# A scan layer without a state between its two chunks, and the decay's differences of three of its groups on ScalarE

## The chip, the cores and the metric

The kernel runs on one core of a Trainium2 chip. A core has engines that each work through a queue of their own in order: TensorE (matmul, "PE" in the profile, its weight loads "PEld"), VectorE ("DVE"), ScalarE ("ACT"), GpSimd ("POOL") and SyncE ("SP", here only the issuer of weight transfers). They wait for one another through semaphores; an instruction that waits holds up everything behind it on its engine. Operands lie in SBUF; TensorE writes into eight PSUM banks of 128 x 512 float32, from which VectorE and ScalarE read.

The metric is device time in microseconds (us) of one execution, as the median of the runs.

## The reference

A decoder trunk of two layers for 256 tokens of width 1024: SwiGLU, a mixer, SwiGLU again, with a layer norm after each. The mixer of the first layer is sparse attention, that of the second a state-space scan (Mamba-2) in two chunks of 128 tokens, 32 heads of 64 in four groups that share B and C (128 states). Only the scan is touched:

```python
xdt = x * dt                                   # (chunk, token, group, head, 64)
a_cs = cumsum(dt * a)                          # within the chunk
decay = exp(where(tril, a_cs[l] - a_cs[s], -inf))
cb = einsum('bclgn,bcsgn->bcgls', cm, bm)
y_diag = einsum('bcgrls,bcsgrp->bclgrp', cb * decay, xdt)
states = einsum('bclgn,bclgrp->bcgrpn', bm, xdt * decay_to_end)
prev = scan of the states over the chunks      # zero for the first chunk
y_off = einsum('bclgn,bcgrpn->bclgrp', cm, prev) * exp(a_cs)
y = y_diag + y_off
```

With two chunks only the second has a nonzero `prev`, and it is the state of the first. So `y_off` of the second chunk is C2 (B1' X1), where B1' X1 is the state and X1 is `xdt * decay_to_end` of the first chunk. The same numbers come from (C2 B1') X1.

## The kernel before

Weights are streamed as 512 KB tiles: SyncE loads them, ScalarE rounds each into a high half (`wh`, L327, or L325 with a scale) and VectorE forms the rest (`wl`, L352, or L349); TensorE multiplies with both. Up to ten tiles are ready ahead of their use. The order on every engine is written by hand: instructions are queued as the Python code calls them.

The scan layer is the function `ssd`. It first projects z, B and C (`z0`, `z_half`, `bc_tile`), then transposes B (`b_tr`, L1467) and multiplies C with B for both chunks (`cb`, L1473). Then it loops over four groups of eight heads (L1636). A tile of x comes from `xs_tile` (a projection, then a conv of one ScalarE instruction, L1449, and three VectorE ones, L1452, and a silu, L1444). For a group g and a chunk t:

- `x_tok` transposes x into tokens and multiplies with dt (L1523, `y[t]`, tile `xdt`) and with the skip factor (L1524, tile `xtok`); `x_end` (L1528) gives X1, tile `xe`.
- `decay_load` broadcasts the cumulated sums into `M` by a transfer of GpSimd; `decay_seg` (L1499) subtracts each of eight heads' column sum, 128 x 128 at a time, and clips at zero, on VectorE; `decay_exp` (L1502) is one exp of 128 x 1024 on ScalarE; `decay_cb` (L1506) multiplies with C times B on VectorE. The `seg`, `exp` and `cb` of group g + 1 are queued in the last part of group g.
- `diag` (L1534) is the diagonal product; `state` (L1540) forms the state from the transposed B (`btok`) and X1 and copies it to SBUF on ScalarE (L1542); `carry` (L1546) multiplies it with C2, and VectorE adds it (L1547, L1548).
- `gate` (L1551, L1552) adds the skip part and multiplies with silu(z); `square`, `root`, `norm` (L1556, L1559, L1563) are the group's RMS norm; `y_tr` (L1568) transposes y on TensorE, and `split_psum` (L526, L527) makes its two halves, `yH` on ScalarE and `yL` on VectorE.

Between these steps stand eight fillers f[0] to f[7], pieces of TensorE work for the next group: x tiles, halves of z, or pieces of the output product. `diag`, `carry`, the second `x_tok` and `y_tr` share two PSUM banks (`ptr`).

Of the kernel before, what the change touches and what calls it, by code (L numbers as in the profile page):

```python
# [408 lines left out]
def trunk_kernel(ctx: ExitStack, tc: tile.TileContext, widths, forms, x, ln_g, ln_b, wts, kvg, convp,  # L409
                 dt_bias, a_log, d_skip, norm_g, out):  # L410
    nc = tc.nc
# [10 lines left out]
    def nm(s):  # L422
        cnt[0] += 1
        return f"{s}_{cnt[0]}"

    def f4(s):
        return wk.tile([128, 1024], F32, name=nm(s), tag="f4", bufs=12)

    def f2(s):
        return wk.tile([128, 512], F32, name=nm(s), tag="f2", bufs=9)  # L430
# [18 lines left out]
    def pspare(n):  # L449

        spare[0] = (spare[0] + 1) % (n + 2)
        if spare[0] < 2:
            return pmm()
        a, b = divmod(spare[0] - 2, 2)
        return psum.tile([128, 512], F32, name=nm("psp"), tag=f"acc{a}{b}", bufs=1)

    def ptr():
        return psum.tile([128, 512], F32, name=nm("ptr"), tag="ptr", bufs=2)
# [20 lines left out]
    ident = consts.tile([128, 128], F32, name="ident")  # L479
# [850 lines left out]
    def ssd(xT, u, ln_i):  # L1330
# [108 lines left out]
        bT, cTt = f4("bT"), f4("cTt")  # L1439
# [22 lines left out]
            W.pump(1 + i % 2)  # L1462

        cbm = f4("cbm")
        btok = f2("btok")

        def b_tr():  # L1467
            pt = pspare(4)
            for g in range(SG):
                nc.tensor.transpose(pt[:, g * 128:(g + 1) * 128], bT[:, g * 256:g * 256 + 128], ident)  # L1470
            nc.scalar.copy(btok, pt)

        def cb(t):  # L1473
            pt = pspare(4)
# [15 lines left out]
        def decay_seg(t, g, on_act=False):  # L1490

            m = M[t, g]
            for h in range(8):
                hs = slice(h * 128, (h + 1) * 128)
                a = acs[t][:, g * 8 + h:g * 8 + h + 1]
                if on_act:
                    nc.scalar.activation(m[:, hs], m[:, hs], AF.Relu, bias=a, scale=-1.0)
                else:
                    nc.vector.tensor_scalar(m[:, hs], m[:, hs], a, 0.0, op0=ALU.subtract, op1=ALU.min)  # L1499

        def decay_exp(t, g, on_act=False):
            nc.scalar.activation(M[t, g], M[t, g], AF.Exp, scale=-1.0 if on_act else 1.0)  # L1502
# [4 lines left out]
                                 .to_broadcast([128, 8, 128]))  # L1507

        yT = {}
        y, xd, xe, st, ss = {}, {}, {}, {}, {}  # L1510

        def x_tok(t, g):

# [21 lines left out]
                                 y[t][:, h * 64:(h + 1) * 64], start=True, stop=True)  # L1535
            return py

        def state(g):
            pst = ptr()
            nc.tensor.matmul(pst, btok[:, g * 128:(g + 1) * 128], xe[g], start=True, stop=True)  # L1540
            st[g] = f2("st")
            nc.scalar.copy(st[g], pst)  # L1542

        def carry(g):
            po = ptr()
            nc.tensor.matmul(po, cTt[:, g * 256 + 128:g * 256 + 256], st[g], start=True, stop=True)  # L1546
            nc.vector.tensor_mul(hv(xe[g]), hv(po), hb(eacs, g))  # L1547
            nc.vector.tensor_add(xd[1], xd[1], xe[g])  # L1548

# [69 lines left out]
        for i in range(4):  # L1619
            xs_tile(0, i, u + i)  # L1620
            if i == 0:
                b_tr()
                cb(0)
                cb(1)
        decay_seg(0, 0)
# [10 lines left out]
        for g in range(SG):  # L1636
            if g < 2:
                f = [lambda i=i: xs_tile(g + 1, i, u + i) for i in range(4)]
                f += [lambda t=t, i=i: (z_half(g + 2, t, i, u + 4), W.pump(1)) for t in range(2) for i in range(2)]
            elif g == 2:  # L1640
                x3 = [lambda i=i: xs_tile(3, i, u + 2 * i) for i in range(4)]
                o0 = [lambda i=i: out_piece(i, u + 2 * i + 1) for i in range(4)]
                f = [x3[0], x3[1], o0[0], x3[2], o0[1], x3[3], o0[2], o0[3]]
            else:
                f = [lambda i=i: out_piece(4 + i, u + i) for i in range(6)]
            f[0]()
            if g:
                x_tok(0, g)
                x_tok(1, g)
            else:  # L1650
                decay_cb(0, 0)
                decay_cb(1, 0)
            x_end(g)
            f[1]()
            f[2]()
            py[0] = diag(0, g)
            state(g)
            gate(0, g, py[0])
            if g < 3:
                decay_load(0, g + 1)  # L1660
            f[3]()
            carry(g)
            square(0)
            root(0)
            py[1] = diag(1, g)
            gate(1, g, py[1])
            if g < 3:
                decay_load(1, g + 1)
            f[4]()
            square(1)  # L1670
            root(1)
            norm(0)
            if g < 3:
                decay_seg(0, g + 1)
            f[5]()
            y_tr(0, g)
            norm(1)
            if g < 3:
                decay_seg(1, g + 1)
                f[6]()  # L1680
                flush()
                y_tr(1, g)
                decay_exp(0, g + 1)
                decay_exp(1, g + 1)
                f[7]()
                decay_cb(0, g + 1)
                decay_cb(1, g + 1)
                W.lows()
                u += 8
# [56 lines left out]
```

## Time and profile before

| what | us |
|---|---|
| median of 3 runs (lowest, highest) | 1030.28 (1030.23, 1030.36) |
| span of the profiled execution (first to last instruction) | 1029.3 |
| TensorE busy in the span | 1014.3 |
| VectorE busy | 882.6 |
| ScalarE busy | 637.4 |
| from the first group's x tiles to the last group's second y_tr, about | 696 to 829 |

The profiled execution's own time isn't listed apart from its span; the median of the runs is 1.0 us above the span, and that is taken as what lies around it. "Busy" is an engine's time in instructions; matmuls overlap, so that a row's duration is longer than the distance to the next row's start, and the same holds for VectorE and ScalarE, by some 0.1 us. In the order of time a row gives start, duration, engine, source line, operation, written tile <- read tiles, shape and count; brackets give how long the engine was idle just before and what ended that.

### The profile page before, as it was taken

To read this page: it belongs to the slowest core of one execution; us is meant where nothing else is said; L and a number is where in the kernel's file an instruction comes from. 1 tells how busy PE (TensorE), PEld (TensorE's weight loads), DVE (VectorE), ACT (ScalarE), POOL (GpSimd) and SP (SyncE) were. 2 spreads that over 40 slices of the span, in tenths; PEclk is the share of its full clock that TensorE was granted. 3 is DMA by queue.
4 is the path that set the end of the run, shared out by engine and by line. 5 is a ranking of instruction groups with operands and counts; after the bars stand their busy time and mean duration, and the time that the engine had idled before them with its cause. 6 is when DMAs were issued, how large, how long until landed. Compare 5 with 4: busy or idle time off the path is not lost.

```text
span 1029.3 us, 14864 instructions
## 1 busy us (share of the span) xinstructions
PE 1014.3 (99%) x5427; PEld 861.6 (84%) x5427; DVE 882.6 (86%) x1305; ACT 637.4 (62%) x977; POOL 94.8 (9%) x152
## 2 busy tenths in 40 slices
PE   8999999999999999999999999999999999999996
PEld 7888888888788888888888888999888888888885
DVE  5889997799799799978978997799999878898984
ACT  6666675476657666754666664586766547566760
POOL 2011000100000010000001000140111110101001
PEclk9999999999999999999999999999999999999998
DMA  9769998352658677884777787355555656678741
GB/s 328 289 142 287 268 330 291 105 172 75 203 186 243 182 201 234 307 305 133 236 205 191 246 295 255 138 170 185 181 167 193 213 207 222 150 234 278 208 156 41
DMA packets 60776, 217.55 MB, mean 211 GB/s; under 512 B 6848, under 2 KB 6912, under 8 KB 60704
## 3 DMA queue, kind: packets, MB, share of 16 engines
q1 hardware_dynamic: 51264, 183.43, 50.5%
q0 software_dynamic: 9152, 32.66, 15.3%
q8 instruction: 42, 0.69, 0.3%
q10 hardware_dynamic: 288, 0.52, 0.1%
q14 instruction: 30, 0.25, 0.1%
HBM read 193.48 MB, written 1.08 MB: 189 GB/s over the span
## 4 chain that ended last, share of the span: by engine, by line
PE 93%; DVE 4%; DMA 1%; ACT 0%; POOL 0%; issue 0%; SPq 0%; POOLq 0%; DVEq 0%
PE pmm L532 11%; PE pmm L530 11%; PE pmm L531 11%; PE acc L530 10%; PE acc L532 10%; PE acc L531 9%; PE pmm L679 4%; PE ptr L679 4%; PE ptr L681 2%; PE pmm L681 2%; PE ptr L531 1%; PE ptr L532 1%; PE pxs L530 1%; PE ptr L530 1%; PE pxs L532 1%; PE pxs L531 1%
## 5 line engine op out<-in xcount | busy, mean ns | idle before, releaser
L352 DVE TENSOR_TENSOR wl<-raw,wh 128x1024 fp32r<-128x1024 f32 (+2 forms) x404 | 475.4, 1212 | 16.0 <-ACT wh L327 15.6
L327 ACT CAST wh<-raw 128x1024 fp32r<-128x1024 f32 (+2 forms) x406 | 407.4, 1045 | 100.8 <-DVE raw L294 46.6
L530 PE MATMUL acc<-wh,hH 128*128 128x512 f32 (+1 forms) x352 | 137.7, 391 | 0.0
L532 PE MATMUL acc<-wh,hL 128*128 128x512 f32 (+1 forms) x352 | 136.6, 388 | 0.0
L531 PE MATMUL acc<-wl,hH 128*128 128x512 f32 (+1 forms) x352 | 136.6, 388 | 0.0
L530 PE MATMUL pmm<-wh,xT 128*128 128x512 f32 (+2 forms) x288 | 114.6, 398 | 0.0
L531 PE MATMUL pmm<-wl,xT 128*128 128x512 f32 (+2 forms) x288 | 110.8, 385 | 0.8 <-DVE wl L352 0.8
L532 PE MATMUL pmm<-wh,xT 128*128 128x512 f32 (+2 forms) x288 | 111.2, 386 | 0.2 <-DVE xT L527 0.2
L532 PEld LDWEIGHTS acc<-wh,hL 128*128 128x128 f32 x352 | 66.1, 188 | 13.7
L530 PEld LDWEIGHTS acc<-wh,hH 128*128 128x128 f32 x352 | 66.2, 188 | 12.7
L531 PEld LDWEIGHTS acc<-wl,hH 128*128 128x128 f32 x352 | 66.2, 188 | 12.6
L532 PE MATMUL pmm<-wh,xf 128*128 128x512 f32 x192 | 74.8, 389 | 0.0
L530 PE MATMUL pmm<-wh,xf 128*128 128x512 f32 x192 | 74.7, 389 | 0.0
L531 PE MATMUL pmm<-wl,xf 128*128 128x512 f32 x192 | 74.7, 389 | 0.0
L267 POOL DMA_DIRECT2D raw<-raw x42 | 36.5, 869 | 410.3 <-DVE raw L294 149.6
L294 DVE TENSOR_TENSOR raw<-raw,raw 128x1024 f32<-128x1024 f32 x54 | 65.2, 1219 | 0.4
L532 PEld LDWEIGHTS pmm<-wh,xT 128*128 128x128 f32 x288 | 54.2, 188 | 12.4 <-DVE xT L527 1.5
L531 PEld LDWEIGHTS pmm<-wl,xT 128*128 128x128 f32 x288 | 54.4, 189 | 10.7 <-DVE wl L352 1.4
L530 PEld LDWEIGHTS pmm<-wh,xT 128*128 128x128 f32 x288 | 54.3, 189 | 9.3 <-ACT wh L327 0.4
L679 PE MATMUL pmm<-xT,wh 128*128 128x512 f32 x192 | 49.3, 399 | 0.0
L679 PE MATMUL ptr<-xT,wh 128*128 128x512 f32 x192 | 47.9, 392 | 0.0
L530 PE MATMUL pxs<-xT,wh 128*128 128x256 f32 x160 | 46.4, 290 | 0.0
(313 smaller groups left out, 1897.6 us busy)
## 6 DMA issues: line engine op xcount, KB each, us to landing
raw<-in_wts_dram SPq DMA_DIRECT2D x339, 512.0 KB, 5.1
raw<-raw POOLq DMA_DIRECT2D x42, 512.0 KB, 5.2
M<-scr POOLq DMA_DIRECT2D x8, 512.0 KB, 5.1
lng<-in_ln_g_dram POOLq DMA_DIRECT2D x6, 512.0 KB, 5.1
lnb<-in_ln_b_dram POOLq DMA_DIRECT2D x6, 512.0 KB, 6.3
raw<-in_wts_dram SPq DMA_DIRECT2D x4, 408.0 KB, 5.3
out_dram<-x SPq DMA_DIRECT2D x4, 256.0 KB, 2.1
raw<-in_wts_dram SPq DMA_DIRECT2D x2, 492.0 KB, 4.8
```

The costliest lines, as they stand in the source:

```text
L267: self.nc.gpsimd.dma_start(self.raw[r], self.raw[other], accum_op=ALU.add)
L294: self.nc.vector.tensor_add(self.raw[r], self.raw[r], self.raw[other])
L327: nc.scalar.copy(h[:, c:c + n], raw[:, c:c + n])
L352: self.nc.vector.tensor_sub(lo[:, s], raw[:, s], h[:, s].bitcast(F32))
L530: nc.tensor.matmul(ps, lh, rh, start=first, stop=False, skip_group_check=on)
L531: nc.tensor.matmul(ps, lh, rl, start=False, stop=False, skip_group_check=on)
L532: nc.tensor.matmul(ps, ll, rh, start=False, stop=last, skip_group_check=on)
L679: nc.tensor.matmul(ps, H[:, k * 128:(k + 1) * 128], xT.HL[:, k, :], start=k == 0, stop=False)
L681: nc.tensor.matmul(ps[:, :SEQ], L[:, k * 128:(k + 1) * 128], xT.H[:, k, :], start=False, stop=k == DK - 1)
```

## The change

The state goes. Instead of transposing B of the first chunk, TensorE multiplies it with C of the second, once for all four groups (`cb_cross`), and ScalarE copies the result to SBUF (`cbx`). `carry` then multiplies `cbx` with X1, so that `state` (a matmul of 128 x 512 and a ScalarE copy per group) is left out. And for groups 2 to 4 (g + 1 in the loop) the eight differences of a chunk are computed on ScalarE, as Relu(a - M) with the sums as a bias; the exp then takes a scale of -1. Both functions had that path (`on_act`) already. Group 1 stays on VectorE.

```diff
         cbm = f4("cbm")
-        btok = f2("btok")
-
-        def b_tr():
+        cbx = f2("cbx")
+
+        def cb_cross():
             pt = pspare(4)
             for g in range(SG):
-                nc.tensor.transpose(pt[:, g * 128:(g + 1) * 128], bT[:, g * 256:g * 256 + 128], ident)
-            nc.scalar.copy(btok, pt)
+                nc.tensor.matmul(pt[:, g * 128:(g + 1) * 128], bT[:, g * 256:g * 256 + 128],
+                                 cTt[:, g * 256 + 128:g * 256 + 256], start=True, stop=True)
+            nc.scalar.copy(cbx, pt)
...
-        def state(g):
-            pst = ptr()
-            nc.tensor.matmul(pst, btok[:, g * 128:(g + 1) * 128], xe[g], start=True, stop=True)
-            st[g] = f2("st")
-            nc.scalar.copy(st[g], pst)
-
         def carry(g):
             po = ptr()
-            nc.tensor.matmul(po, cTt[:, g * 256 + 128:g * 256 + 256], st[g], start=True, stop=True)
+            nc.tensor.matmul(po, cbx[:, g * 128:(g + 1) * 128], xe[g], start=True, stop=True)
...
             if i == 0:
-                b_tr()
+                cb_cross()
                 cb(0)
                 cb(1)
...
             py[0] = diag(0, g)
-            state(g)
             gate(0, g, py[0])
...
             norm(0)
             if g < 3:
-                decay_seg(0, g + 1)
+                decay_seg(0, g + 1, True)
             f[5]()
             y_tr(0, g)
             norm(1)
             if g < 3:
-                decay_seg(1, g + 1)
+                decay_seg(1, g + 1, True)
                 f[6]()
                 flush()
                 y_tr(1, g)
-                decay_exp(0, g + 1)
-                decay_exp(1, g + 1)
+                decay_exp(0, g + 1, True)
+                decay_exp(1, g + 1, True)
```

Three places in the queues show what moves. The first is ScalarE at the end of group 1, from the first norm on (`xdt` is y, `zs` silu of z, `wh` a weight tile's high half, `M` the decay). Before:

```order
L1563 ACTIVATE xdt_7128<-xdt_7128,rs_7332 128x512
L1430 ACTIVATE zs_7394<-pmm_7347 128x512
L327 CAST wh_7399<-raw_7263 128x1024
L526 CAST yH_7407<-ptr_7402 128x512
L1563 ACTIVATE xdt_7137<-xdt_7137,rs_7371 128x512
L327 CAST wh_7436<-raw_7318 128x1024
L1444 ACTIVATE xsT_7310<-cv_7311 128x256
L526 CAST yH_7445<-ptr_7440 128x512
L1502 ACT_TABLE_LOAD
L1502 ACTIVATE M_7283<-M_7283 128x1024
```

In the changed kernel the same stretch reads:

```order
L1558 ACTIVATE xdt_7128<-xdt_7128,rs_7328 128x512
L1498 ACTIVATE M_7279<-M_7279,acs_6849 128x128 x8
L1430 ACTIVATE zs_7390<-pmm_7343 128x512
L327 CAST wh_7395<-raw_7263 128x1024
L526 CAST yH_7403<-ptr_7398 128x512
L1558 ACTIVATE xdt_7137<-xdt_7137,rs_7367 128x512
L1498 ACTIVATE M_7341<-M_7341,acs_6851 128x128 x8
L327 CAST wh_7432<-raw_7314 128x1024
L1444 ACTIVATE xsT_7306<-cv_7307 128x256
L526 CAST yH_7441<-ptr_7436 128x512
L1503 ACT_TABLE_LOAD
L1503 ACTIVATE M_7279<-M_7279 128x1024
```

Eight instructions of 128 x 128 stand behind each of the two norms; nothing else has changed its place, and the number of table loads is the same. The second place is VectorE at the same point of the program, from the root of the second chunk to the products with C times B. Before:

```order
L1559 TENSOR_SCALAR ss_7366<-ss_7366 128x1
L1499 TENSOR_SCALAR M_7283<-M_7283,acs_6849 128x128 x8
L352 TENSOR_TENSOR wl_7364<-raw_7225,wh_7363 128x1024
L527 TENSOR_TENSOR yL_7408<-ptr_7402,yH_7407 128x512
L1499 TENSOR_SCALAR M_7345<-M_7345,acs_6851 128x128 x8
L352 TENSOR_TENSOR wl_7400<-raw_7263,wh_7399 128x1024
L527 TENSOR_TENSOR yL_7446<-ptr_7440,yH_7445 128x512
L352 TENSOR_TENSOR wl_7437<-raw_7318,wh_7436 128x1024
L1506 TENSOR_TENSOR M_7283<-M_7283,cbm_6374 128x1024
L1506 TENSOR_TENSOR M_7345<-M_7345,cbm_6374 128x1024
L352 TENSOR_TENSOR wl_7468<-raw_7361,wh_7467 128x1024
```

And in the changed kernel:

```order
L1554 TENSOR_SCALAR ss_7362<-ss_7362 128x1
L352 TENSOR_TENSOR wl_7360<-raw_7225,wh_7359 128x1024
L527 TENSOR_TENSOR yL_7404<-ptr_7398,yH_7403 128x512
L352 TENSOR_TENSOR wl_7396<-raw_7263,wh_7395 128x1024
L527 TENSOR_TENSOR yL_7442<-ptr_7436,yH_7441 128x512
L352 TENSOR_TENSOR wl_7433<-raw_7314,wh_7432 128x1024
L1507 TENSOR_TENSOR M_7279<-M_7279,cbm_6374 128x1024
L1507 TENSOR_TENSOR M_7341<-M_7341,cbm_6374 128x1024
L352 TENSOR_TENSOR wl_7464<-raw_7357,wh_7463 128x1024
```

The two runs of eight are gone; what is left reads, row by row, something that ScalarE has just written (`wh`, `yH`, `M`). The third place is TensorE behind the first diagonal product of group 1 (`pxs` is the next x tile). Before:

```order
L532 MATMUL pxs_7230<-xT_6313,wl_6892 128x256
L1534 MATMUL ptr_7268<-xdt_7128,M_6853 128x64 x8
L1540 MATMUL ptr_7277<-xe_7190,btok_6375 128x512
L530 MATMUL pxs_7285<-xT_6313,wh_6928 128x256
L531 MATMUL pxs_7285<-xT_6313,wh_6928 128x256
```

And in the changed kernel:

```order
L532 MATMUL pxs_7230<-xT_6313,wl_6892 128x256
L1535 MATMUL ptr_7268<-xdt_7128,M_6853 128x64 x8
L530 MATMUL pxs_7281<-xT_6313,wh_6928 128x256
L531 MATMUL pxs_7281<-xT_6313,wh_6928 128x256
L532 MATMUL pxs_7281<-xT_6313,wl_6929 128x256
```

The state product has left the queue, and the x tile follows the diagonal directly; `carry` keeps its place behind the x tile.

More of the change, by code (lines that the diff above doesn't have):

```diff
@@ L1509, in ssd @@
         yT = {}
-        y, xd, xe, st, ss = {}, {}, {}, {}, {}
+        y, xd, xe, ss = {}, {}, {}, {}
         def x_tok(t, g):
```

## The prediction

> **What bounds the kernel now.** I read the page first, then the waits of TensorE, then the order of time engine by engine between 690 and 830 us, the stage that the change touches. The first row is the page's busy time (us, share of the span, instructions); the next two are rows of the waits (who waited for whom, us in total, times, longest); the fourth is ten microseconds of that stage (PE, PEld, DVE, ACT, POOL busy, then clock).
>
> ```profile
> PE 1014.3 (99%) x5427; PEld 861.6 (84%) x5427; DVE 882.6 (86%) x1305; ACT 637.4 (62%) x977; POOL 94.8 (9%) x152
> ...
> PE ptr L1534 <- DVE xdt L1551: 0.8, 1, 0.8
> ...
> PE pxt L1521 <- ACT xsT L1444: 0.7, 1, 0.7
> ...
> 740.00:750.00 10.00, 10.00 (x79) 9.68 (x78) 9.24 (x13) 8.75 (x11) 0.00 (x0) 1.00 0.60 196
> ```
>
> TensorE is the bound: 1.5 us of waits in the whole scan layer, both in its first group. So an instruction taken from TensorE is worth its time, but only as long as VectorE (9.24 of 10 us) and ScalarE (8.75 of 10) keep up. ScalarE's 62% is an average; in this window it is nearly full, and the change adds to it there.
>
> **Term 1, TensorE's instructions.** Rows of the chain of work (start, us, what):
>
> ```profile
> 696.26 0.44 PE psp L1470 x4
> 696.70 1.91 PE pmm L1477 x16
> ...
> 782.68 0.91 PE ptr L1540 x2
> ```
>
> The state product of a group (L1540) goes: 0.91 us each, four times, 3.64 us. The four transposes (0.44 us) become four products of the form of L1477, which are two instructions each: 1.91 / 8 = 0.24 us each, 0.96 in all, so +0.52. The fourth now needs the last C tile, which a ScalarE row dates (start, us):
>
> ```profile
> 696.76 0.41 ACT L1444 ACTIVATE cTt<-cv 128x256 f32<-128x256 f32 x1
> ```
>
> The tile is ready at 697.17, the fourth product would start at 696.98: about 0.2 more. TensorE, then VectorE behind it, are on the chain until group 1's second diagonal, so this +0.7 is paid in full.
>
> **Term 2, the moved differences.** Eight 128x128 VectorE instructions (row 735.00 below) take 1.65 us; ScalarE has no Relu of 128x128 in this trace. The nearest form is L1166: same size, in place, a per-partition bias, scale -1 (its accumulator read is a row of its own):
>
> ```profile
> 231.00 0.39 ACT L1166 ACTIVATE lg<-lg,mx 128x128 f32<-128x128 f32 x1
> 231.29 0.19 ACT L1166 ACTIVATION_READ_ACCUMULATOR lg<-lg,mx 128x1 f32 x1
> ```
>
> The next instruction starts 0.29 us after it. Bounds: 0.18 (in the rows below a silu of 512 columns without a bias pointer starts its successor after 0.50 us and a cast of 1024 after 0.93; that slope leaves 0.18 for 128) and 0.39 (no overlap at all). I take 0.29, the row of the same form: eight are 2.3 us, sixteen 4.6 us per group, for groups 2 to 4. The removed state copy (0.58 us of ScalarE) lies where ScalarE waits anyway: nothing.
>
> Where they stand decides. Group 1's end on ScalarE:
>
> ```profile
> 734.54 0.71 ACT L1563 ACTIVATE xdt<-xdt,rs 128x512 f32<-128x512 f32 x1
> 735.36 0.60 ACT L1430 ACTIVATE zs<-pmm 128x512 f32<-128x512 f32 x1
> 735.86 1.04 ACT L327 CAST wh<-raw 128x1024 fp32r<-128x1024 f32 x1
> 736.79 0.59 ACT L526 CAST yH<-ptr 128x512 fp32r<-128x512 f32 x1
> 737.27 0.74 ACT L1563 ACTIVATE xdt<-xdt,rs 128x512 f32<-128x512 f32 x1
> ...
> 744.92 1.04 ACT L327 CAST wh<-raw 128x1024 fp32r<-128x1024 f32 x1
> ```
>
> From the first norm to the cast at 744.92 ScalarE has only some 0.3 us of gaps, so sixteen more instructions push that cast by 4.4 us. VectorE and TensorE behind it (start, us, what, and in brackets the idle time before):
>
> ```profile
> 735.00 1.65 DVE L1499 TENSOR_SCALAR M<-M,acs 128x128 f32<-128x128 f32 x8
> ...
> 745.99 1.23 DVE L352 TENSOR_TENSOR wl<-raw,wh 128x1024 fp32r<-128x1024 f32 x1 [0.69 <-ACT wh L327]
> ...
> 748.56 0.68 DVE L1523 TENSOR_TENSOR xdt<-pxt,dt 128x512 f32<-128x512 f32 x1
> ...
> 756.72 0.69 DVE L1551 TENSOR_TENSOR xdt<-ptr,xtok 128x512 f32<-128x512 f32 x1
> ...
> 778.47 0.68 DVE L1523 TENSOR_TENSOR xdt<-pxt,dt 128x512 f32<-128x512 f32 x1
> ...
> 785.28 0.69 DVE L1551 TENSOR_TENSOR xdt<-ptr,xtok 128x512 f32<-128x512 f32 x1
> ```
>
> ```profile
> 727.80 2.00 PE L1534 MATMUL ptr<-xdt,M 128*128 128x64 f32 x16 [0.75 <-DVE xdt L1551]
> 738.57 0.60 PE L1568 MATMUL ptr<-ident,xdt 128*128 128x128 f32 x4
> ...
> 757.62 1.89 PE L1534 MATMUL ptr<-xdt,M 128*128 128x64 f32 x16
> ...
> 768.22 0.60 PE L1568 MATMUL ptr<-ident,xdt 128*128 128x128 f32 x4
> ```
>
> Times below are those of before; "+" is how much later an event comes, the 0.7 of term 1 apart.
>
> Group 1. First norm ends 735.17 as now. Eight Relus to 737.5, then silu 0.49, cast 0.93, yH 0.47: the second norm starts at 739.4 and ends at 740.1. The transposes of y(1) stand at 738.57 and need it: **+1.6** on TensorE. Eight more Relus and the rest unchanged: the cast of 744.92 comes at 749.3. VectorE is 3.2 us lighter but does not get ahead: it waits in program order for yH(1), for both exponentials, then for that cast, as it does already (0.69 us in brackets at 745.99). So L1523 comes at 752.9, +4.4, and the 8.2 us from there to L1551 hold no idle time: gate(0) also +4.4. The second diagonal of group 2 waits for it (its bank is the one that gate(0) reads): now it starts 0.2 us after L1551 ends at 757.41, so **+4.2**. The state product taken out of TensorE before it buys only a wait, here as in group 1, where the row at 727.80 waits for L1551 already.
>
> Group 2 has the same tail:
>
> ```profile
> 764.21 0.71 ACT L1563 ACTIVATE xdt<-xdt,rs 128x512 f32<-128x512 f32 x1
> ...
> 774.17 0.60 ACT L1430 ACTIVATE zs<-pmm 128x512 f32<-128x512 f32 x1
> ```
>
> Its norm hangs on VectorE, +4.4. Relus (769.2 to 771.5), silu, a cast of 1.04, yH: the second norm ends at 774.3, so y(1)'s transposes of 768.22 come **+6.1**. After the next eight Relus, the table load and the exponentials the silu of 774.17 ends at 783.5. TensorE's next x tile uses the PSUM bank that it reads:
>
> ```profile
> 775.09 0.36 PE L530 MATMUL pmm<-xT,wh 128*128 128x256 f32 x1
> ...
> 787.32 1.73 PE ptr L1534 x16
> ...
> 797.92 0.57 PE ptr L1568 x4
> ```
>
> That is **+8.4**. VectorE's L1523 of 778.47 is +8.8, gate(0) of 785.28 ends at 794.8; TensorE, 0.91 us earlier without the state, meets it within 0.1: the diagonal of 787.32 comes +7.6.
>
> Group 3: VectorE had 0.4 us of idle time and regains it, so its norm is +8.4. ScalarE had a gap before the conv of the last tile:
>
> ```profile
> 787.10 1.51 DVE L1452 SCALAR_TENSOR_TENSOR cv<-pmm,convp_sb,cv 128x255 f32<-128x255 f32 x3 [0.41 <-ACT cv L1449]
> ...
> 794.77 0.56 ACT L1449 ACTIVATE cv<-pmm,convp_sb 128x256 f32<-128x256 f32 x1 [0.74 <-PE pmm L532]
> ```
>
> That gap takes 0.74 of the 2.3 us: the second norm and y(1)'s transposes of 797.92 come **+10.0**. In group 4 the gate is early:
>
> ```profile
> 812.05 0.69 DVE L1551 TENSOR_TENSOR xdt<-ptr,xtok 128x512 f32<-128x512 f32 x1
> ```
> ```profile
> 816.56 1.73 PE ptr L1534 x16
> ```
>
> It ends 3.8 us before the diagonal that needs it, so VectorE's delay is covered there and the last state is a true 0.91 less: +9.1. What follows is a TensorE queue without waits.
>
> **Sum**: 9.1 + 0.7 = +9.8 us on a span of 1029.3. The median of the runs, 1030.28, lies 1.0 above that span, so the forecast is **1040.1 us**. With 0.18 or 0.39 us per Relu the same steps give +4.7 or +13.1 for 9.1, so 1035.6 to 1044.1.
>
> [...]
>
> **Rivals.** (a) The clock. Its granted value at the end of the program (the column after POOL):
>
> ```profile
> 1019.00:1020.00 1.00, 0.73 (x7) 0.52 (x5) 0.23 (x1) 0.00 (x0) 0.00 (x0) 1.00 0.00 0
> ...
> 1022.00:1023.00 1.00, 0.00 (x0) 0.00 (x0) 0.54 (x2) 0.00 (x0) 0.82 (x1) 0.50 0.00 0
> ```
>
> It halved within 2.3 us of the last matmul (1019.73 to 1022.0). My steps leave TensorE idle for 2.7 us (before 757.62) and 2.3 us (before 775.09), the others under 2.1. At the start of the program matmuls sped up as follows:
>
> ```profile
> 4.86 1.12 PE L548 MATMUL pxT<-ident,x 128*128 128x128 f32 x4 [1.04 <-DMA x<-in_x_dram]
> ...
> 7.12 0.78 PE L530 MATMUL pmm<-wh,xT 128*128 128x512 f32 x1
> ...
> 8.08 0.40 PE L532 MATMUL pmm<-wh,xT 128*128 128x512 f32 x1
> ```
>
> From 4.86, where work became dense, to 8.0 it ran slowly: 3.2 us at half speed lose 1.6. Two such gaps give 1043.3. [...]
>
> (b) The delay does not add up over groups: VectorE's 3.2 us per group make up for it between L1523 and the gate. Then only the transposes of y(1) wait, 1.6, 1.7 (+6.1 behind a norm that is +4.4) and 2.0 us, less 0.91 three times, plus 0.7: +3.3, 1033.6. Against it: that stretch is work released by TensorE and by in-order ScalarE.
>
> (c) Faster: the Relus cost TensorE nothing, and three states go: 0.7 - 2.7 = -2.0, 1028.3. It decides at the cast of 744.92: only if the sixteen Relus delay it by under about 0.7 us does gate(0) hide it. For it: ScalarE is only 62% busy over the span. Against it: none of that idle time lies between the first norm and that cast.
>
> **Chances.** Forecast 0.60; clock 0.15; (b) 0.12; (c) 0.10; nothing visible 0.03. A measurement of this kernel tells about 0.2% (2.1 us) from no change, and (c) lies at that bound, so half of it counts to each side: slower 0.87, within 0.2% 0.08, faster 0.05. Range 1033 to 1044: forecast with its Relu bounds, (b), (a); left out are (c), no change and a clock that falls three times.
>
> **What would show it.** In the trace of the changed kernel: eight Relus in 2.3 us; TensorE waiting for the norm before y(1)'s transposes (1.6 us), for gate(0)'s add before group 2's second diagonal (2.7), for the silu before the x tile (2.3); VectorE idle behind exponentials and casts; clock at 1.00. If VectorE's L1523 of group 2 comes less than 2 us later, or ScalarE starts the Relus before its norm, the forecast is wrong.

## The result, and the profile after

| | us |
|---|---|
| changed kernel, median of 4 runs (lowest, highest) | 1042.37 (1041.71, 1043.58) |
| kernel before beside it (lowest, highest) | 1030.32 (1030.23, 1030.53) |
| ratio, 95% interval | 1.0116 (1.0102 to 1.0131) |
| changed kernel once more, beside the experiments | 1041.52 (1041.22, 1043.40), ratio 1.0110 (1.0094 to 1.0126) |
| forecast (range) | 1040.1 (1033 to 1044) |

The change makes the kernel slower by 12.05 us in the first set and by 10.85 in the second (1041.52 less 1030.67, the kernel before beside it); +9.8 was forecast. The page of the changed kernel, its busy times and, below them, who TensorE waited for (us in total, times, longest):

```profile
PE 1020.2 (98%) x5423; PEld 868.1 (83%) x5423; DVE 873.5 (84%) x1257; ACT 649.5 (62%) x1021; POOL 96.5 (9%) x152
PE ptr L1535 <- DVE xdt L1546: 3.9, 2, 2.3
PE pmm L530 <- ACT zs L1430: 2.0, 1, 2.0
PE ptr L1563 <- ACT xdt L1558: 1.4, 1, 1.4
```

VectorE has 9.1 us less to do and ScalarE 12.1 more. TensorE has 3.1 us less work by term 1 (3.64 less 0.52), and yet it is busy for 5.9 us longer: that points at its clock. The kinds of wait are the ones that were named ahead: the gate before the second diagonal (L1535; the 3.9 us are 1.61 in group 1 and 2.32 in group 2), the silu before an x tile (L530), the norm before y(1)'s transposes (L1563). One stands elsewhere: the norm was to be waited for in group 1 (1.6 us), and here TensorE waits for it in group 3 alone. In groups 1 and 2 it comes to these transposes later than forecast, for a reason that follows below.

ScalarE in the changed kernel around group 1's end, in the order of time (start, duration; brackets: idle before, and what ended it). Compare it with the same stretch of before, where the norm of 734.54 was followed by the silu at 735.36 and the last of these casts stood at 744.92:

```profile
734.96 0.70 ACT L1558 ACTIVATE xdt<-xdt,rs 128x512 f32<-128x512 f32 x1
735.57 2.44 ACT L1498 ACTIVATE M<-M,acs 128x128 f32<-128x128 f32 x8
739.00 0.60 ACT L1430 ACTIVATE zs<-pmm 128x512 f32<-128x512 f32 x1 [0.99 <-PE pmm L532]
...
741.53 2.44 ACT L1498 ACTIVATE M<-M,acs 128x128 f32<-128x128 f32 x8
743.87 1.04 ACT L327 CAST wh<-raw 128x1024 fp32r<-128x1024 f32 x1
...
750.83 1.04 ACT L327 CAST wh<-raw 128x1024 fp32r<-128x1024 f32 x1
```

Eight Relus push the next instruction by 743.87 - 741.53 = 2.34 us: 0.29 each, the estimate. VectorE in the same kernel, behind that last cast:

```profile
751.90 1.22 DVE L352 TENSOR_TENSOR wl<-raw,wh 128x1024 fp32r<-128x1024 f32 x1 [1.43 <-ACT wh L327]
...
754.47 0.68 DVE L1524 TENSOR_TENSOR xdt<-pxt,dt 128x512 f32<-128x512 f32 x1
```

It idles behind the cast (1.43 us, 0.69 before), and its product for group 2 starts at 754.47, where it started at 748.56.

The clock was 1.00 in this stage before, in every half microsecond from 690 to 850. Now (windows of the changed kernel: start:end, us, busy PE, PEld, DVE, ACT, POOL, then the granted clock):

```profile
731.00:733.00 2.00, 2.00 (x5) 1.54 (x6) 1.93 (x5) 0.00 (x0) 0.07 (x1) 0.50 0.25 49
...
766.00:769.00 3.00, 3.00 (x10) 2.61 (x11) 2.89 (x6) 0.00 (x0) 0.82 (x3) 0.50 0.44 139
...
787.00:790.00 3.00, 3.00 (x17) 3.00 (x16) 2.69 (x5) 1.69 (x3) 0.62 (x1) 0.54 0.00 0
```

The rows lie in three stretches at half clock, and each of these begins at the end of one of TensorE's waits or some 1.0 us behind it. Read in narrow windows, they reach from 729.24 to 736.06, from 763.37 to 770.20 and from 787.26 to 790.68: 6.8, 6.8 and 3.4 us. Half of these 17 us is lost to TensorE, 8.5 us by this estimate, and its busy time is 9.0 longer than term 1 alone would make it (5.9 and 3.1). In the first row above TensorE counts as fully busy and yet gets through 5 matmuls in 2 us. The silu's wait of 0.99 us at 739.00 comes from the same loss: in experiment 8, whose clock stays up, the silu follows the Relus without a wait (ScalarE is busy for all 4.00 us from 736 to 740).

### The profile page after: what moved, and what is told of

It is laid out like the page before. It is cut to its first block, busy times and chain, and to the rows that moved or that the text cites. A ratio compares the mean times of both kernels' runs of the same rounds, so it can differ in the third digit from the quotient of the medians.

```text
span 1041.9 us, 14849 instructions
## 1 busy us (share of the span) xinstructions
PE 1020.2 (98%) x5423; PEld 868.1 (83%) x5423; DVE 873.5 (84%) x1257; ACT 649.5 (62%) x1021; POOL 96.5 (9%) x152
## 4 chain that ended last, share of the span: by engine, by line
PE 89%; DVE 6%; ACT 3%; issue 1%; POOL 0%; DMA 0%; POOLq 0%; DVEq 0%
PE pmm L532 11%; PE pmm L530 11%; PE pmm L531 11%; PE acc L530 9%; PE acc L532 9%; PE acc L531 9%; PE pmm L679 4%; PE ptr L679 4%; PE ptr L681 2%; PE pmm L681 2%; PE ptr L530 1%; PE ptr L532 1%; PE ptr L531 1%; DVE wl L352 1%; PE ptr L1535 1%; PE pxs L530 1%
## 5 line engine op out<-in xcount | busy, mean ns | idle before, releaser
L530 PE MATMUL acc<-wh,hH 128*128 128x512 f32 (+1 forms) x352 | 137.7, 391 | 0.0
L530 PE MATMUL pmm<-wh,xT 128*128 128x512 f32 (+2 forms) x288 | 116.5, 405 | 0.0
L532 PE MATMUL pmm<-wh,xT 128*128 128x512 f32 (+2 forms) x288 | 113.0, 392 | 0.2 <-DVE xT L527 0.2
L530 PEld LDWEIGHTS acc<-wh,hH 128*128 128x128 f32 x352 | 66.2, 188 | 12.7
L530 PE MATMUL pmm<-wh,xf 128*128 128x512 f32 x192 | 74.8, 389 | 0.0
L532 PEld LDWEIGHTS pmm<-wh,xT 128*128 128x128 f32 x288 | 55.2, 192 | 12.7 <-DVE xT L527 1.5
L530 PEld LDWEIGHTS pmm<-wh,xT 128*128 128x128 f32 x288 | 55.6, 193 | 9.4
L530 PE MATMUL pxs<-xT,wh 128*128 128x256 f32 x160 | 45.8, 286 | 0.0
```

What stands on the lines that cost most here:

```text
L530: nc.tensor.matmul(ps, lh, rh, start=first, stop=False, skip_group_check=on)
L532: nc.tensor.matmul(ps, ll, rh, start=False, stop=last, skip_group_check=on)
```

## The experiments

Each kernel was timed beside the kernel before on the same chip; "before" in brackets is its median there.

**1. The state's removal alone.** The changed kernel with the differences back on VectorE:

```diff
-                decay_seg(0, g + 1, True)
+                decay_seg(0, g + 1)
...
-                decay_exp(0, g + 1, True)
+                decay_exp(0, g + 1)
```
(and the same for chunk 1)

> The changed kernel with the decay's differences of groups 2 to 4 back on VectorE, so that of the two parts of the change only the removed state is left. Theory (the Relus on ScalarE cost nearly all, the state is worth its 0.91 us only where TensorE does not wait right behind it): +0.7 from the C times B products in the chain, nothing saved in group 1 (the second diagonal waits for gate(0) already, 0.75 us), little in groups 2 and 3, 0.91 saved in group 4: 1028.5 to 1031, most likely 1030.1, no difference that can be measured from 1030.3; no half-clock stretch, or one in group 1, where TensorE's wait before the second diagonal grows from 0.75 to about 1.7 us; one would add about 1 us. Rival A (the state's removal itself makes the kernel slower, by the longer waits and the clock): 1034 or more. Rival B (each removed state counts in full): 1030.3 + 0.7 - 3.6 = 1027.4.

Measured: 1031.50 us (before 1030.97), ratio 1.0005 (0.9995 to 1.0015): no difference that can be told, and no net gain from 3.6 us of TensorE instructions taken away. It did lose its clock in group 1. The second diagonal's row, a window behind it, and the scan layer's last transposes of y(1), which experiment 7 takes up:

```profile
729.06 2.10 PE L1535 MATMUL ptr<-xdt,M 128*128 128x64 f32 x16 [1.61 <-DVE xdt L1546]
```
```profile
731.00:733.00 2.00, 2.00 (x6) 1.61 (x6) 1.97 (x4) 0.43 (x1) 0.00 (x0) 0.50 0.12 41
```
```profile
829.33 0.60 PE L1563 MATMUL ptr<-ident,xdt 128*128 128x128 f32 x4
```

The ten executions run from 1029.53 to 1032.91 us; they follow the mean granted clock of the execution: 0.997 in the two fastest (1029.53, 1030.08), 0.994 in the slowest, 0.995 or 0.996 between. Rival A (1034 or more) and rival B (1027.4) are out.

**2. The Relus alone.** The kernel before, with the differences of groups 2 to 4 on ScalarE:

```diff
-                decay_seg(0, g + 1)
+                decay_seg(0, g + 1, True)
...
-                decay_exp(0, g + 1)
+                decay_exp(0, g + 1, True)
```

> The kernel before with the differences of groups 2 to 4 on ScalarE, and the state kept. Theory (the Relus stand ahead of the norms and of the cast in ScalarE's order): +10 us, 1040 to 1042; TensorE waits for the norm before y(1)'s transposes in group 1 (1.4 us), for gate(0)'s add before group 2's second diagonal (about 1.5, since the state product fills 0.9 of it), for the silu before an x tile (about 2). In group 1 TensorE's wait before the second diagonal stays at 0.75 us, so the half-clock stretch there should be gone while those behind the longer waits may stay. Rival (the Relus are cheap by themselves and only the two parts together, through the clock, make it slower): under 1035.

Measured: 1041.60 us (before 1030.97), ratio 1.0107 (1.0092 to 1.0122). TensorE's waits in it:

```profile
PE ptr L1568 <- ACT xdt L1563: 4.4, 3, 1.5
PE pmm L530 <- ACT zs L1430: 2.1, 1, 2.1
PE ptr L1534 <- DVE xdt L1551: 1.6, 2, 0.9
```

All three are of the expected kinds. The norm and the x tile have the expected size; the wait for the gate before group 2's second diagonal is 0.87 us instead of 1.5, with another 0.71 us ahead of that group's first diagonal. The clock falls only behind the 2.1 us before the x tile (0.67 from 784 to 788 us, 0.91 from 788 to 792, and 1.00 in the other windows from 688 to 848). The moved differences alone are as slow as the whole change (ratio 1.0110 in the second set): beside them, no gain from the removed states can be told.

**3. The same Relus, eight of them earlier.** In the changed kernel, the first eight of a group stand ahead of the square of y(1):

```diff
+            if g < 3:
+                decay_seg(0, g + 1, True)
             square(1)
             root(1)
             norm(0)
-            if g < 3:
-                decay_seg(0, g + 1, True)
```

> The changed kernel, with the first eight Relus of each group queued ahead of the square of y(1) on ScalarE, where that engine waits for VectorE (2.6 to 3.7 us idle in the kernel before); same instructions, same number. Place theory (it is where the Relus stand, ahead of a norm on which TensorE waits, and not their number): the first eight fall into idle time, y(1)'s transposes wait no more, the cast behind comes some 2.3 us later instead of 4.4 per group: 1034 to 1037. Cost theory (sixteen Relus per group cost ScalarE time wherever they stand): no change, 1041 to 1043. If the early Relus wait themselves for something that is late, they hold up the square and it gets slower than 1042.

Measured: 1038.57 us (before 1030.97), ratio 1.0080 (1.0065 to 1.0095): faster than the change with the same instructions, but short of what the place theory expected. Two rows of ScalarE show what it had left out, and one of TensorE, below them, bears on the clock:

```profile
737.68 0.60 ACT L1430 ACTIVATE zs<-pmm 128x512 f32<-128x512 f32 x1 [1.71 <-PE pmm L532]
...
807.62 2.45 ACT L1498 ACTIVATE M<-M,acs 128x128 f32<-128x128 f32 x8 [2.03 <-DMA M<-scr]
```
```profile
762.06 2.00 PE L1535 MATMUL ptr<-xdt,M 128*128 128x64 f32 x16 [2.32 <-DVE xdt L1546]
```

In group 1 the silu waits for a TensorE at half clock; in group 3 the second eight wait for the transfer that loads their input. Experiment 10 takes the first of these away. The clock fell twice in this profile, behind the 1.60 us wait in group 1 (matmuls of 128x512 take 0.63 us there up to 733.54 and 0.39 from 734.28) and the x tile's of 2.54 us in group 3 (those of 128x256 take 0.41 us up to 784.98 and 0.28 from 785.39), but not behind the third row's 2.32 us: that diagonal took 2.00 us, where in the changed kernel, behind a wait of the same length at the same place, it took 3.68.

**4. Two waits filled.** The changed kernel, with the product in `carry` repeated, so that TensorE works while it would wait:

```diff
-            nc.tensor.matmul(po, cbx[:, g * 128:(g + 1) * 128], xe[g], start=True, stop=True)
+            for _ in range((2, 3, 1, 1)[g]):
+                nc.tensor.matmul(po, cbx[:, g * 128:(g + 1) * 128], xe[g], start=True, stop=True)
```

> The changed kernel, with the inter-chunk product (C times B, times xe) of groups 1 to 4 issued 2, 3, 1 and 1 times, so that TensorE works in its waits for gate(0) before the second diagonals of groups 1 and 2 (0.46 us a product for 128x512 by estimate from 0.91 for two passes). The result is the same, the repeated products overwrite each other. Clock theory (the waits of 1.6 and 2.3 us there let the clock fall to half for 3.4 to 6.8 us, each worth about 1 us): the half-clock stretches behind these two waits vanish, that behind the x tile's wait for the silu stays: 1040 to 1041. Rival (the half clock costs nothing, since TensorE waits for the other engines right behind it): 1041.5 to 1043 although the clock stays up. Second rival (the added products themselves delay the gate): over 1043.

Measured: 1041.61 us, lowest to highest 1041.46 to 1041.79 (before 1030.97). The clock is 1.00 behind both filled waits (727 to 735 and 763 to 767 us) and still falls behind the x tile's (0.60 from 784 to 788). But the time is below the first set of the changed kernel only, not below the second, and it lies in the rival's range (1041.5 to 1043), not in the clock theory's (1040 to 1041): the next section shows why, since these two falls cost nothing in the second set's profile. The spread of the four executions is 0.3 us instead of 2.

**5 and 6. One group at a time.** The differences on ScalarE only for group 2, as below, and only for group 4, with `g == 2` there:

```diff
-                decay_seg(0, g + 1, True)
+                decay_seg(0, g + 1, g == 0)
```

> The changed kernel with the differences of group 2 alone on ScalarE (those of groups 3 and 4 back on VectorE). Additive theory (each group's sixteen Relus push that group's cast and with it the next gate, and the delay stays): the +4.2 us of the second diagonal of group 2 in full on the 1031.5 of the kernel without any Relus, and a second half-clock stretch behind the longer wait there: 1035 to 1036.5. Rival A (later groups make up for the delay): under 1033.5. Rival B (every group costs the same third of the whole, 3.6 us): 1035.1, which only the next run tells from the theory.

> The changed kernel with the differences of group 4 alone on ScalarE. Theory (what is paid depends on what is late behind the Relus: in group 3 the gate that follows is early by 3.8 us, so only the first eight cost, through the norm for which y(1)'s transposes wait): 1031.5 for the kernel without any Relus, plus 1.5: 1032.5 to 1033.5. Rival (every group costs a third of the whole, 3.6 us): 1035.1. Rival (nothing, the gap of 0.74 us before the last conv and the early gate take it): 1031.5.

Measured: group 2 alone 1037.23 us (1036.11 to 1037.63), group 4 alone 1033.11 (1031.51 to 1034.82), before 1030.76. The groups don't cost the same, which was the point: over the kernel without any Relus (1031.50, another set), group 2 costs 5.7 us and group 4 only 1.6 as expected; with each time taken over its own kernel before it is 5.9 and 1.8. Group 2 came out 0.7 us above the additive theory's upper end. Its profile, taken on the fastest of its executions (1036.11), agrees with the theory: counted from the first L1470 row, the last transposes of y(1) come 4.26 us later than in experiment 1's profile (137.12 less 132.86), against the forecast's +4.2. What made the other three 1.1 to 1.5 us slower isn't on record. With group 4 alone, TensorE waits for the norm ahead of group 3's y(1) and for nothing else that is new:

```profile
800.53 0.66 PE L1563 MATMUL ptr<-ident,xdt 128*128 128x128 f32 x4 [1.73 <-ACT xdt L1558]
```

Its ten executions fall into three sets: four at 1031.5 to 1031.7 us with a mean clock of 0.997 or 0.998, five at 1033.0 to 1033.4 with 0.995 or 0.996, one at 1034.82 with 0.993. The steps between the sets are 1.6 us, about what half clock for 3.4 us loses (1.7). In the one profile, of 1032.98 us, the clock falls once, for 3.4 us, behind group 1's wait of 1.60 us: the diagonal there takes 2.44 us, and matmuls of 128x512 take 0.63 us up to 732.03 and 0.39 from 732.85. That this wait cost nothing in four executions and twice as much in one is read from times and mean clocks; they have no profile.

**7. The clock alone.** Experiment 1 with `carry`'s product of group 1 issued twice (`range((2, 1, 1, 1)[g])`).

> The kernel with the state removed and all differences on VectorE, and the inter-chunk product of group 1 issued twice, so that TensorE's wait before the second diagonal of group 1 falls from 1.61 us to some 0.75. Clock theory (a wait of 1.6 us lets the clock fall, one of 0.75 doesn't): no half-clock stretch in the scan layer, 0.5 to 1 us less than the 1031.5 without the repeat, a narrower spread: 1030.5 to 1031. Rival (the fall of the clock costs nothing here, TensorE's lost time lies beside waits): 1031.5, clock at 1.00.

Measured: 1029.90 us (1029.52 to 1030.38; before 1030.76), ratio 0.9993 (0.9985 to 1.0002). One more product on TensorE, and 1.2 us less against the kernel before (by the two ratios, whose intervals overlap a little); that is below the expected 1030.5 to 1031. The row and the window to hold against those of experiment 1, and the last transposes of y(1):

```profile
728.77 2.00 PE L1535 MATMUL ptr<-xdt,M 128*128 128x64 f32 x16 [0.75 <-DVE xdt L1547]
```
```profile
731.00:733.00 2.00, 2.00 (x11) 1.62 (x10) 1.97 (x3) 0.14 (x1) 0.00 (x0) 1.00 0.03 10
```
```profile
827.47 0.60 PE L1564 MATMUL ptr<-ident,xdt 128*128 128x128 f32 x4
```

The wait is 0.75 us instead of 1.61, the clock stays at 1.00, 11 matmuls pass in the 2 us instead of 6, and no execution is above 1030.38, where eight of experiment 1's ten are above 1031. Counted from the first L1470 row of their own profile (696.18 here, 696.47 there), the last transposes of y(1) come at 131.29 instead of 132.86: the fall had cost 1.57 us, and all of it had reached the end. So the rival (the clock's fall costs nothing here) is out. In the kernel before they come at 132.10; by these profiles the state's removal is therefore worth 0.8 us with the clock up, which the fall had hidden; the times (ratio 0.9993, 0.9985 to 1.0002) can't tell so little from nothing. Experiment 1 ran on another chip, but the kernel before lies between 1029.99 and 1031.20 us on both.

**8 and 9. All three waits filled, and the changed kernel beside it.** To experiment 4 comes, in `x_tok`:

```diff
-            for i in range(4):
+            for i in list(range(4)) * (5 if t and g == 2 else 1):
                 nc.tensor.transpose(pt[:, i * 128:(i + 1) * 128], xsT[g][i][:, t * 128:(t + 1) * 128], ident)
```

> The kernel with the repeated inter-chunk products, and in group 3 the four transposes of the second chunk's x issued five times (0.44 us each, the same bank and the same result), so that TensorE also works in its 2.1 us wait for the silu before the x tile. Clock theory: no half-clock stretch in the scan layer, the first diagonal of group 3 starts 1 to 1.5 us earlier than the 99.80 us behind the first C times B product that it has in the kernel with two waits filled, and about 0.9 of that reaches the end: 1040.4 to 1041.0, and what is left over 1030.3 is the ladder of waits alone, +9.9 to +10.5. Rival (that stretch lies beside VectorE's later gate and costs nothing): 1041.6, clock at 1.00. Second rival (the repeats delay VectorE's read of the bank): 1042 or more.

> The changed kernel itself, unchanged, beside the kernel with all three waits filled. Clock theory: 1 to 2 us above that one, 1042 to 1042.5 in the median, and a wider spread (1041.7 to 1043.6 before), since how long the clock stays at half differs between executions. Rival (the clock costs nothing): within 0.5 us of it, with the same spread.

Measured: 1041.15 us (1040.90 to 1041.25) with the waits filled, 1041.52 (1041.22 to 1043.40) without; before 1030.67. (The 99.80 us in the expectation is a slip: 95.63 is what the kernel with two waits filled has.) The first diagonal of group 3 comes 94.27 us behind the first L1470 row, 1.4 earlier, and y(1)'s last transposes 0.85 earlier, both as the clock theory had it; the time is 0.15 us above its range, and 10.48 above its own kernel before, at the upper end of the expected ladder. For the changed kernel beside it the clock theory had 1 to 2 us more: the median is only 0.4 above, which fits its rival, while the spread (2.2 us instead of 0.35) does not. The filled kernel's clock, at the two places where it fell last:

```profile
766.00:769.00 3.00, 3.00 (x14) 2.45 (x14) 2.89 (x7) 0.00 (x0) 1.19 (x3) 1.00 0.53 175
...
787.00:790.00 3.00, 3.00 (x18) 2.44 (x17) 2.93 (x7) 2.22 (x5) 0.62 (x1) 1.00 0.39 146
```

So this is the changed kernel's work with its clock up, and the steps of the forecast can be read from it (next section). In the medians of this set the clock is worth 0.4 us (the intervals of the two ratios overlap), between the slowest executions 2.2; against the first set's median it is worth 1.6 (12.05 less 10.48).

**10. Early Relus with the clock up.** Experiments 3 and 8 together.

> The kernel with all three of TensorE's waits filled, and the first eight Relus of each group ahead of the square of y(1) on ScalarE. The kernel with these Relus early and no filled wait gave 1038.6 where 1034 to 1037 was expected; there the silu of group 1 waited 1.71 us for a TensorE at half clock, and the second eight Relus of groups 2 and 3 waited 0.65 and 2.03 us for the load of their decays. Place theory with the clock as what was missed: only the second eight push the casts, by some 2.2 us in each of groups 1 and 2, y(1)'s transposes wait under 0.5 us: 1034 to 1036. Rival (the load of the decays holds the second eight in any case): 1036.5 to 1038.5. Cost theory (the number of Relus alone counts): 1041.

Measured: 1037.25 us (before 1030.36), ratio 1.0068 (1.0051 to 1.0085): the first rival. Over its own kernel before it is 6.9 us slower, where experiment 8 is 10.5 slower over its own; so moving eight of each sixteen Relus is worth 3.6 us, and place counts and not number alone (the clock is 1.00 in every window from 688 to 848 us); but the second eight now wait, in every group, for the load of their sums, in the order of ScalarE:

```profile
739.59 2.46 ACT L1498 ACTIVATE M<-M,acs 128x128 f32<-128x128 f32 x8 [0.76 <-DMA M<-scr]
...
772.38 2.46 ACT L1498 ACTIVATE M<-M,acs 128x128 f32<-128x128 f32 x8 [0.62 <-DMA M<-scr]
...
805.87 2.45 ACT L1498 ACTIVATE M<-M,acs 128x128 f32<-128x128 f32 x8 [2.04 <-DMA M<-scr]
```

**11. A version that beats both.** Experiment 1 with the four C times B products moved from the head of the scan layer to behind the first diagonal of group 1, ahead of TensorE's wait there:

```diff
             if i == 0:
-                cb_cross()
                 cb(0)
...
             py[0] = diag(0, g)
+            if not g:
+                cb_cross()
             gate(0, g, py[0])
```

> A version meant to beat both: the state removed, all differences on VectorE, and the four C times B products moved from the head of the scan layer to behind the first diagonal of group 1, where TensorE waits 1.6 us for gate(0) afterwards. Theory: they leave the chain there (the 0.9 us by which the first diagonal stood later), TensorE's wait falls under 1 us and the clock stays up, the rest of the state's removal counts only where TensorE doesn't wait (group 4, 0.9 us): 1029 to 1030. Rival A (carry(0) waits for the copy of the products behind ScalarE's casts, and VectorE's gate(1) with it): 1031 or more. Rival B (the whole removal counts once the clock stays up): under 1028.5.

Measured: 1028.89 us (1028.63 to 1029.67; before 1030.76), ratio 0.9983 (0.9974 to 0.9992): 1.9 us faster than the kernel before, just under the expected 1029 to 1030, with the clock at 1.00. On TensorE the products now stand at 722.04, and the wait behind them is 0.71 us:

```profile
722.04 1.11 PE L1470 MATMUL pmm<-cTt,bT 128*128 128x128 f32 x8
...
727.61 2.00 PE L1535 MATMUL ptr<-xdt,M 128*128 128x64 f32 x16 [0.71 <-DVE xdt L1546]
```

The copy that `carry` needs stands in time among ScalarE's casts (rival A is out):

```profile
724.61 0.58 ACT L1472 COPY cbx<-pmm 128x512 f32<-128x512 f32 x1
```

## Where the prediction was right and wrong

Slower, within the range, and through the kinds of wait that were named; the sum was 2.3 us low in the first set and 1.4 in the second. The range had room for that, since it allowed for rival (a) and for a dearer Relu; the sum itself had no such term. What can be checked is more than the sum: each step was a delay of a certain matmul. The rows below give starts on TensorE, first those of the kernel before that the prediction doesn't show:

```profile
696.10 0.60 PE L1470 MATMUL psp<-ident,bT 128*128 128x128 f32 x4
...
787.16 1.89 PE L1534 MATMUL ptr<-xdt,M 128*128 128x64 f32 x16
797.83 0.66 PE L1568 MATMUL ptr<-ident,xdt 128*128 128x128 f32 x4
...
828.20 0.60 PE L1568 MATMUL ptr<-ident,xdt 128*128 128x128 f32 x4
```

The same steps in the changed kernel (first profile):

```profile
695.62 0.83 PE L1470 MATMUL psp<-cTt,bT 128*128 128x128 f32 x6
696.74 0.49 PE L1470 MATMUL psp<-cTt,bT 128*128 128x128 f32 x2 [0.29 <-ACT cTt L1444]
728.21 2.77 PE L1535 MATMUL ptr<-xdt,M 128*128 128x64 f32 x16 [1.61 <-DVE xdt L1546]
741.99 0.60 PE L1563 MATMUL ptr<-ident,xdt 128*128 128x128 f32 x4
763.37 3.68 PE L1535 MATMUL ptr<-xdt,M 128*128 128x64 f32 x16 [2.32 <-DVE xdt L1546]
777.16 0.60 PE L1563 MATMUL ptr<-ident,xdt 128*128 128x128 f32 x4
798.96 1.89 PE L1535 MATMUL ptr<-xdt,M 128*128 128x64 f32 x16
811.11 0.66 PE L1563 MATMUL ptr<-ident,xdt 128*128 128x128 f32 x4 [1.39 <-ACT xdt L1558]
840.63 0.60 PE L1563 MATMUL ptr<-ident,xdt 128*128 128x128 f32 x4
```

And in the kernel with all three waits filled (experiment 8), whose clock stayed up:

```profile
696.34 0.83 PE L1470 MATMUL psp<-cTt,bT 128*128 128x128 f32 x6
728.93 2.00 PE L1535 MATMUL ptr<-xdt,M 128*128 128x64 f32 x16 [0.74 <-DVE xdt L1547]
741.30 0.66 PE L1564 MATMUL ptr<-ident,xdt 128*128 128x128 f32 x4 [1.46 <-ACT xdt L1559]
762.99 2.00 PE L1535 MATMUL ptr<-xdt,M 128*128 128x64 f32 x16 [0.60 <-DVE xdt L1547]
775.46 0.66 PE L1564 MATMUL ptr<-ident,xdt 128*128 128x128 f32 x4 [1.54 <-ACT xdt L1559]
796.12 1.89 PE L1535 MATMUL ptr<-xdt,M 128*128 128x64 f32 x16
808.75 0.66 PE L1564 MATMUL ptr<-ident,xdt 128*128 128x128 f32 x4 [1.82 <-ACT xdt L1559]
838.32 0.60 PE L1564 MATMUL ptr<-ident,xdt 128*128 128x128 f32 x4
```

Each start is taken from the first L1470 row of its own kernel (the stage begins up to 1.1 us earlier or later in one execution than in another), and the kernel before's is subtracted; so 741.30 - 696.34 less 738.57 - 696.10 is +2.49. The forecast's column has its 0.7 of term 1 in it.

| TensorE step | forecast | waits filled | changed kernel |
|---|---|---|---|
| group 1, second diagonal | +0.7 | +0.89 | +0.89 |
| group 1, y(1)'s transposes | +2.3 | +2.49 | +3.90 |
| group 2, second diagonal | +4.9 | +5.13 | +6.23 |
| group 2, y(1)'s transposes | +6.8 | +7.00 | +9.42 |
| group 3, second diagonal | +8.3 | +8.72 | +12.28 |
| group 3, y(1)'s transposes | +10.7 | +10.68 | +13.76 |
| group 4, y(1)'s transposes | +9.8 | +9.88 | +12.91 |

- **Term 2, the moved differences**: right, in its place, its price (0.29 us a Relu) and its whole chain, to 0.4 us at every step, as long as the clock is up. There TensorE does wait for the norm before y(1)'s transposes of group 1, for 1.46 us. One wait on the way was worked out wrongly, though no step hangs on it: the 2.7 us before group 2's second diagonal are about the difference of two steps (4.2 less 1.6), without the 0.91 of the state product that is gone. In the changed kernel the wait there is 2.32 us, with another of 0.44 ahead of the group's first diagonal. The fall from the sixth row to the last is the group in which the gate is early and the removed state counts.
- **Term 1, the state**: right in direction and a little too small. The four products and their wait for the last C tile (0.29 us) put group 1's second diagonal 0.9 us later instead of 0.7. That the removed state "buys only a wait" in groups 1 and 2 is what experiment 1's waits show (1.61 instead of 0.75 us, and a new one of 0.67). Where TensorE doesn't wait it counts: experiment 7, whose clock is up, gains 0.8 us by its profile, too little for its times to tell.
- **The clock**: this is the step that failed. The sum held the clock at 1.00 and rival (a) let it fall behind two waits, of 2.7 and 2.3 us; "the others under 2.1" were taken to be safe. It fell to 0.50 behind three, of 1.61, 2.32 and 2.0 us. The one that was not counted is in group 1, and it is the state's removal that made it: without the state's product, TensorE's wait there grows from 0.75 us to 1.61. Experiments 7 and 8 fill the waits and the falls are gone. In size rival (a) had one price, 1.6 us a fall. A fall of 3.4 us did lose that much in experiment 1 (1.57 us), but two falls of the first profile lasted twice as long, and a wait behind a fall can swallow what it lost: three falls gave 3.0 us in the first profile (12.91 - 9.88), where two of them lasted 6.8 us, and 0.9 in the second one, where all three lasted 3.4. Its rows are

```profile
695.69 0.83 PE L1470 MATMUL psp<-cTt,bT 128*128 128x128 f32 x6
...
774.81 0.66 PE L1563 MATMUL ptr<-ident,xdt 128*128 128x128 f32 x4
...
838.57 0.60 PE L1563 MATMUL ptr<-ident,xdt 128*128 128x128 f32 x4
```

(838.57 - 695.69 less 132.10 is +10.78). In that one the first two falls cost nothing: group 2's transposes of y(1) stand at 774.81 - 695.69 = 79.12, as in the filled kernel (775.46 - 696.34), where TensorE waits 1.54 us for the norm in front of them. The lower clock used up that wait, so it cost only what the next wait didn't swallow.

- **Rival (b)**, that the delay doesn't add up, is out by the table (the 2.0 us that it has for group 3 are worked out nowhere; the forecast's own steps give 1.6, from 8.4 to 10.0); **rival (c)**, that the Relus cost TensorE nothing, by experiment 2. Group 1's cast came 6.4 us later (750.83 - 695.62 less 744.92 - 696.10). In the filled kernel it came 5.3 later: 0.9 of it term 1 and 4.4 the Relus, as forecast; the other 1.1 is the clock.
- Of the experiments' own misses, the early Relus missed their 1034 to 1037 in part by the clock, in part by the load of the sums, which the prediction had no need to price. Group 2 alone came out 0.7 us above its range; in its profile the clock fell behind the 2.32 us before group 2's second diagonal (matmuls of 128x512 take 0.63 us up to 767.62 and 0.39 from 768.97). That longer falls made up the rest is likely, but not shown.

What stays open: the kernel with all waits filled is 10.5 us above its kernel before in the medians, and the table accounts for 9.9 of it. The profiled span begins its scan layer 0.2 us later, the rest is not told apart from the difference between executions.

## What to carry to other kernels

An instruction taken from the bounding engine is worth its time only where that engine doesn't wait right behind it; otherwise it turns into a longer wait, and a longer wait of TensorE can cost clock (1.61 us did in experiment 1, 0.75 us in experiment 7 didn't). So put the work that a change adds on TensorE into such a wait (experiment 11), and ask of work moved to an engine with idle time on average what stands behind it in that engine's order: 24 Relus early or late were worth 3.6 us, all 48 of them some 10. Follow such a delay from engine to engine, matmul by matmul, rather than by busy shares: 62% here hid nothing.

## What the hardware showed that was not expected

- TensorE's clock fell to half behind waits of 1.6 us, in some executions only, by their times: with the same program (experiment 6), ten executions lay in three sets 1.6 us apart, with mean clocks of 0.997 or 0.998, 0.995 or 0.996, and 0.993.
- In the changed kernel's first profile the clock changed at 729.24, 736.06, 763.37, 770.20, 787.26 and 790.68, between 1.00 and 0.50 each time. The distances, 6.82, 27.31, 6.83, 17.06 and 3.42 us, are 2, 8, 2, 5 and 1 times the smallest of them to within 0.05 us. That is one profile; why they are so isn't shown.
- Before group 1's second diagonal TensorE waited 1.60 or 1.61 us in both profiles of the changed kernel and in those of experiments 1, 3 and 6, and the clock fell behind that wait in all five. In the kernel before and in experiments 4, 7, 8, 10 and 11 it waited 0.71 to 0.75 us there, and the clock stayed at 1.00.
- Length alone doesn't decide: in experiment 8 TensorE waited 1.46, 1.54 and 1.82 us for the norm ahead of y(1)'s transposes, and its clock stayed at 1.00, while it fell behind 1.61 us before the diagonal in the profiles of experiment 1 and of the changed kernel. Nor does length and place: behind 2.32 us before group 2's second diagonal it fell in the changed kernel (the diagonal took 3.68 us) and not in experiment 3 (2.00 us). What else decides wasn't tried and stays open.
- The spread was wider where the clock fell: 1029.5 to 1032.9 us in experiment 1, 1029.5 to 1030.4 with one wait filled (experiment 7). Where a kernel's times spread by more than its neighbours', the granted clock is worth a look.
